# Gated linear attention in a two-layer decoder: states of 128-token tiles in place of the scores of the two largest levels

## The chip, the cores and the metric

The kernel runs on one core of a Trainium2 chip. PE (TensorE) multiplies matrices into PSUM, DVE (VectorE) and ACT (ScalarE) work on elements, POOL (GpSimd) fills masks and SP (SyncE) issues most loads. Each engine works through its own instructions in order, and semaphores hold it where data or a buffer is not ready. The metric is the device time of one execution in microseconds, the median of the runs shown.

## The reference

A trunk of two layers on 512 tokens of width 1024: latent attention, then gated linear attention (GLA), each followed by a squared-ReLU MLP of width 4096. Only GLA matters here. It has 4 heads, with 128 key channels and 256 value channels each:

```python
b = cumsum(gk)                                   # log decay, per key channel
o_inter = (q_ * exp(b_)) @ state
attn[t, s] = sum_d q_[t, d] * k_[s, d] * exp(b_[t, d] - b_[s, d])     # s <= t
o_intra = attn @ v_
new_state = state * exp(b_last) + (k_ * exp(b_last - b_)).T @ v_
...
o = rms_norm(o, g_norm) * silu(g)
```

The reference goes by chunks of 64 tokens with a state. In exact arithmetic any division into chunks gives the same output, from scores between all pairs of tokens (no state) to a state after each token.

## The kernel before, in words

Nearly every product is done in three matmuls on a high and a low part of both operands (`mm3`, L109: high by high, high by low, low by high, 32-bit words in the reduced format that the code calls F32R). `split` (L102) makes the two parts: ACT copies the high one, DVE subtracts it from the source for the low one. Products that are not split run in full f32 and leave two matmul records for each instruction. Transposes (`tr`, L128) are PE instructions against an identity.

`gla` (L1008) projects `q`, `k`, `v` and `g` from the normalized input. `q` and `k` stand with channels on partitions and tokens along the row, `v` and `g` with tokens on partitions. `b_type` (L1015) computes a half of `v` or `g`, two heads, into four PSUM banks, one for each tile of 128 tokens; `proj_qk` (L1066) computes two heads of `q` or `k`. `gates` (L1142) takes one head's decays: a matmul (L1144), absolute value, exponential, logarithm on ACT, and on DVE the sums over pairs, fours, and so on, which one exponential turns into the decays `T[m]` of blocks of m tokens, from m = 1 to m = 128.

`levels` (L1176) makes one head's scores with decay, level by level. `grow(m)` multiplies the queries of odd blocks and the keys of even blocks by the neighbour's decay, so that after it queries carry the decay since the start of their block of m tokens and keys the decay to its end. `pairs`, `fours` and `halves` fill the scores inside each tile of 128 tokens (matrix `A`), which `halves(64)` splits into `ADh` and `ADl`. `large(1)` and `large(2)` (L1267) make the scores between tiles: 128 columns for neighbouring tiles (0 to 1, 2 to 3), then 256 columns for tiles 0 and 1 against 2 and 3, in f32, each split into `AOh` and `AOl`. `apply` (L1298) multiplies scores by values: ten tile pairs of three matmuls of 256 columns, for four outputs in two PSUM banks. Each output is squared on ACT with its sum (L1312) and multiplied by the gate `g` on DVE (L1314); `small_rstd` (L273) and L1317 to L1322 scale it. `gather` (L1325) turns it to channel-major, splits it, and the output projection takes it.

The order: `heads` (L1351) yields small stages for heads 0 and 1, then for 2 and 3; each stage's products are issued behind the next stage's preparation. `proj` runs the projections in the order `v g q k G V` (capitals are the second halves, heads 2 and 3), and the loop at L1380 takes `PACE` = 1.27 stages for each unit of projection. The scores of a pair of heads can be made as soon as their `q` and `k` are there; `apply` also waits until their half of `v` and `g` is ready (`ready`, L1365). For heads 2 and 3 this is when the last projection ends, so what is left runs by itself, followed by the output projection (`out_proj`, L776). `gates(2)` and `gates(3)` are called ahead of the first `apply`.

PSUM has eight banks: two of tag "a", three "b", three "c" (L64). `apply` takes its two banks from "a" for even heads, "b" for odd ones; the `q` and `k` projections take "a". Scores, gates and transposes take "c". Work tiles of tag `tmp` have six buffers. Pools hand a buffer on when its last reader is done.

Of the kernel before, what the change touches and what calls it, by code (L numbers as in the profile page):

```python
# [34 lines left out]
HV = 256  # L35
# [15 lines left out]
def trunk_kernel(ctx: ExitStack, tc: tile.TileContext, t_in: dict, out: bass.AP, out_row: bass.AP):  # L51
    nc = tc.nc
    PE, ACT, DVE, POOL, SP = nc.tensor, nc.scalar, nc.vector, nc.gpsimd, nc.sync
# [5 lines left out]
    def uname(s):  # L59
        count[0] += 1  # L60
        return f"{s}_{count[0]}"
# [14 lines left out]
    def bank(tag):  # L76
        return psum["pool"].tile([P, 512], F32, tag=f"ps_{tag}", bufs=psum["banks"][tag], name=uname("ps"))
# [11 lines left out]
    def tmp(shape=(P, 512), dt=F32):  # L89
        return sb.tile(list(shape), dt, tag="tmp", bufs=6, name=uname("tmp"))  # L90
# [8 lines left out]
    def f(ap):  # L99
        return ap.bitcast(F32)  # L100

    def split(src, hi, lo, hi_eng=ACT, lo_eng=DVE, order=lambda i: i):  # L102
        if hi_eng is ACT:
            order(ACT.activation(hi, src, AF.Copy))  # L104
        else:
            hi_eng.tensor_copy(hi, src)
        lo_eng.tensor_tensor(lo, src, f(hi), ALU.subtract)  # L107

    def mm3(psum, w, x, start, stop):  # L109
        wh, wl = w  # L110
        xh, xl = x
        PE.matmul(psum, wh, xh, start=start, stop=False)  # L112
        PE.matmul(psum, wh, xl, start=False, stop=False)  # L113
        PE.matmul(psum, wl, xh, start=False, stop=stop)  # L114
# [6 lines left out]
    def act_e(*a, **k):  # L121
        with tc.issue_after(table[0].ins):
            return ACT.activation(*a, **k)
# [4 lines left out]
    def tr(psum, src):  # L128
        PE.transpose(psum, src, ident[: src.shape[0], : src.shape[0]])  # L129
# [13 lines left out]
    def cut(pair, *idx):  # L143
        return tuple(t[idx] for t in pair)
# [56 lines left out]
    def gcol(name, j):  # L201
        c = GAIN_COL[name] + j
        return gains[:, c : c + 1]
# [18 lines left out]
    class Norm:  # L222
# [30 lines left out]
        def add(self, j, src):  # L253
            self.scaled(j, src)
            self.square(src)
# [752 lines left out]
    def gla(layer, nrm, vtag, ytag):  # L1008
# [4 lines left out]
        gp = es.enter_context(tc.tile_pool(name="gla", bufs=1, reuse_waits="tile"))  # L1013
# [99 lines left out]
        p = bank("a")  # L1113
# [11 lines left out]
        V = [[None, None] for _ in range(NT)]  # L1125
# [16 lines left out]
        def gates(h):  # L1142
            p = bank("c")
            PE.matmul(p, wg[:, h * P : (h + 1) * P], av, start=True, stop=True)  # L1144
            bcol = gcol("bgk", 4 * layer + h)
            l = tmp()
            ACT.activation(l, p, AF.Abs, bias=bcol)
            m_ = tmp()
            DVE.tensor_scalar(m_, p, bcol, 0.0, ALU.add, ALU.min)
# [22 lines left out]
        AT = {}  # L1172
# [3 lines left out]
        def levels(h):  # L1176
            q, both, T, A = qk[h], qk[4 + h], B[h], A_of[h % 2]
            qd, k = both[:, :S], both[:, S:]
            at = AT[h] = {}
# [7 lines left out]
            def grow(m):  # L1187
                if m == 1:
                    DVE.tensor_tensor(qd.rearrange("p (t c) -> p t c", t=NT), q[:, :, :P], T[1].rearrange("p (t c) -> p t c", t=NT), ALU.mult)
# [74 lines left out]
                return products  # L1264


            def large(lev):  # L1267
                pairs = [(0, 0, P, 1), (2, P, P, 3)] if lev == 1 else [(0, 0, 256, 2), (1, 256, 256, 2)]
                width = 256 * lev
                p = bank("c")[:, :width]  # L1270
                for j, c, n, i0 in pairs:
                    PE.matmul(p[:, c : c + n], k[:, j * P : (j + 1) * P], qd[:, i0 * P : i0 * P + n], start=True, stop=True)  # L1272
                ao = tuple(gp.tile([P, width], F32R, tag=f"{x}{lev}", bufs=2, name=uname(x)) for x in ("AOh", "AOl"))
                ACT.activation(ao[0], p, AF.Copy)
                DVE.tensor_tensor(ao[1], p, f(ao[0]), ALU.subtract)
                for j, c, n, i0 in pairs:
                    for r in range(n // P):
                        at[(j, i0 + r)] = cut(ao, slice(None), slice(c + r * P, c + (r + 1) * P))

            yield pairs  # L1280
            for grown, level in (
                ((2,), lambda: fours(2)),
                ((4, 8), lambda: fours(8)),
                ((16, 32), lambda: halves(32)),
                ((64,), lambda: halves(64)),
                ((P,), lambda: lambda: large(1)),
                ((2 * P,), lambda: lambda: large(2)),
            ):
                def stage(grown=grown, level=level):
                    for m in grown:  # L1290
                        grow(m)
                    return level()

                yield stage

        Y = [None] * ND

        def apply(h):  # L1298
            at = AT[h]
            hf, vs = h // 2, slice((h % 2) * HV, (h % 2 + 1) * HV)  # L1300
            banks = [bank("ab"[h % 2]) for _ in range(2)]
            ms = sb.tile([P, NT], F32, tag="gms", bufs=2, name=uname("gms"))
            os_ = []
            for i in range(NT):
                o = banks[i // 2][:, (i % 2) * HV : (i % 2 + 1) * HV]
                for j in range(i + 1):
                    mm3(o, at[(j, i)], cut(V[j][hf], slice(None), vs), j == 0, j == i)
                os_.append(o)
                if i % 2:
                    for r in (i - 1, i):  # L1310
                        sq = tmp((P, HV))
                        ACT.activation(sq, os_[r], AF.Square, accum_out=ms[:, r : r + 1])  # L1312
                        g = G[hf][:, r, h % 2, :]
                        DVE.tensor_tensor(g, os_[r], g, ALU.mult)  # L1314
                    yield
            r = small_rstd(ms, NT, 1.0 / HV)
            for i in range(NT):  # L1317
                g = G[hf][:, i, h % 2, :]
                if i % 2:
                    ACT.activation(g, g, AF.Copy, scale=r[:, i : i + 1])  # L1320
# [30 lines left out]
        def heads():  # L1351
            for h in (0, 2):
                while any(i not in qk for i in (h, h + 1, 4 + h, 5 + h)):
                    yield
                late = None
                for two in zip(levels(h), levels(h + 1)):
                    for stage in two:
                        products = stage()
                        if late:
                            late()  # L1360
                        late = products
                        yield
# [52 lines left out]
    for k0, k1 in ((0, 1), (1, 2), (2, 4), (4, 6), (6, 8)):  # L1415
        w = piece(raw0[:, k0:k1], k1 - k0, KL, tc.keep_in_program_order)
# [160 lines left out]
```

## Time and profile before

| | |
|---|---|
| median of 3 runs | 1086.14 us |
| lowest and highest | 1085.81 and 1086.2 us |
| span of the profiled execution | 1084.4 us |
| PE busy | 1075.7 us (99%) |
| PE weight loads busy | 909.5 us (84%) |
| DVE busy | 859.6 us (79%) |
| ACT busy | 549.2 us (51%) |
| three matmuls of `mm3`, 512 columns, tiles `set`, `wh`, `wl` | 760 each, 390 to 391 ns a record |

Times in the profile are microseconds from the start of the span. A row of a timeline gives start, duration, engine, line, operation, output<-inputs and shapes. A row of a group gives the count, then busy microseconds and mean nanoseconds of one, then idle time before and what ended it. PE records overlap: the next matmul starts 0.23 us after one of 512 columns although each is shown with 0.39, so costs on PE are read from start to start. A row of windows gives the stretch, its length, the busy time of PE, of weight loads, DVE, ACT and POOL (with instruction counts), the granted PE clock, DMA's busy share and GB/s. A row of the chain of waits gives start, time and what set the end there.

### The profile page before, as it was taken

The numbers are of one execution on the slowest core, as the hardware profiler recorded it, in microseconds if no ns is written. First come the engines' busy times: TensorE is split into PE (matmuls) and PEld (weight loads), VectorE is DVE, ScalarE is ACT, GpSimd is POOL, SyncE is SP. The second block draws the span as 40 slices with busy tenths as digits, with TensorE's granted clock in tenths as the row PEclk, the third lists the DMA queues.
The fourth block names the chain that finished last, engine by engine and source line by source line (L and its number), as shares of the span: only waits on it lengthen the run. The fifth ranks groups of instructions, "written<-read, shape, count | busy, mean of one in ns | idle before, by whom it ended". The sixth has DMA issues, their size and how long they took to land.

```text
span 1084.4 us, 14045 instructions
## 1 busy us (share of the span) xinstructions
PE 1075.7 (99%) x5372; PEld 909.5 (84%) x5372; DVE 859.6 (79%) x1426; ACT 549.2 (51%) x927; POOL 43.4 (4%) x72
## 2 busy tenths in 40 slices
PE   9999999999999999999999999999999999999997
PEld 7888888888888888888788888888888888888886
DVE  7899968987887887977686584569888797797875
ACT  7767654553453453455345736556445345344354
POOL 8310002000000000000000000000000000000000
PEclk9999999999999999999999999999999999999999
DMA  7311232142332332322322222232233233223122
GB/s 225 88 50 39 79 117 78 61 134 78 117 117 78 117 117 78 110 84 79 90 76 78 78 78 75 70 127 67 90 115 119 79 101 123 87 80 125 69 97 78
DMA packets 86195, 101.61 MB, mean 94 GB/s; under 512 B 7440, under 2 KB 64016, under 8 KB 86128
## 3 DMA queue, kind: packets, MB, share of 16 engines
q1 hardware_dynamic: 84320, 99.67, 28.5%
q10 hardware_dynamic: 1808, 1.05, 0.3%
q8 instruction: 42, 0.69, 0.3%
q14 instruction: 25, 0.20, 0.1%
HBM read 98.35 MB, written 2.10 MB: 93 GB/s over the span
## 4 chain that ended last, share of the span: by engine, by line
PE 97%; DVE 1%; DMA 0%; ACT 0%; issue 0%; SPq 0%; DVEq 0%; ACTq 0%
PE ps L112 21%; PE ps L114 21%; PE ps L113 21%; PE ps L923 17%; PE ps L924 9%; PE ps L1201 2%; PE ps L129 1%; PE ps L408 1%; PE ps L871 1%; PE ps L1272 0%; PE ps L671 0%; PE ps L1251 0%; PE ps L667 0%; PE ps L670 0%; DMA gains<-in_gains_dram 0%; PE ps L669 0%
## 5 line engine op out<-in xcount | busy, mean ns | idle before, releaser
L112 PE MATMUL ps<-set,wh 128*128 128x512 f32 x760 | 296.8, 391 | 0.0
L113 PE MATMUL ps<-set,wh 128*128 128x512 f32 x760 | 296.6, 390 | 0.0
L114 PE MATMUL ps<-set,wl 128*128 128x512 f32 x760 | 296.3, 390 | 0.0
L104 ACT ACTIVATE wh<-wraw 128x1024 fp32r<-128x1024 f32 x139 | 147.0, 1061 | 240.8 <-PE ps L113 115.2
L107 DVE TENSOR_TENSOR wl<-wraw,wh 128x1024 fp32r<-128x1024 f32 x139 | 169.9, 1222 | 41.8 <-ACT wh L104 41.5
L114 PEld LDWEIGHTS ps<-set,wl 128*128 128x128 f32 x760 | 142.7, 188 | 30.3 <-DVE wl L107 0.2
L112 PEld LDWEIGHTS ps<-set,wh 128*128 128x128 f32 x760 | 142.7, 188 | 29.8
L113 PEld LDWEIGHTS ps<-set,wh 128*128 128x128 f32 x760 | 142.8, 188 | 27.6
L923 PE MATMUL ps<-T,wh 128*128 128x512 f32 x448 | 157.5, 391 | 0.0
L924 PE MATMUL ps<-T,wl 128*128 128x256 f32 x448 | 126.2, 282 | 0.0
L923 PE MATMUL ps<-set,wh 128*128 128x512 f32 x336 | 119.9, 397 | 0.0
L923 PEld LDWEIGHTS ps<-T,wh 128*128 128x128 f32 x448 | 84.1, 188 | 18.2
L924 PE MATMUL ps<-set,wl 128*128 128x256 f32 x336 | 94.2, 280 | 0.0
L107 DVE TENSOR_TENSOR wl<-comb,wh 128x1024 fp32r<-128x1024 f32 x42 | 51.4, 1223 | 47.7 <-ACT wh L104 47.7
L837 DVE TENSOR_TENSOR xT<-ps,xT 128x512 f32<-128x512 f32 x120 | 82.3, 686 | 7.1 <-PE ps L114 7.1
L104 ACT ACTIVATE wh<-comb 128x1024 fp32r<-128x1024 f32 x42 | 44.6, 1061 | 83.2 <-PE ps L923 81.8
L924 PEld LDWEIGHTS ps<-T,wl 128*128 128x128 f32 x448 | 84.6, 189 | 0.5
L923 PEld LDWEIGHTS ps<-set,wh 128*128 128x128 f32 x336 | 63.1, 188 | 15.1
L941 DVE TENSOR_TENSOR tmp<-ps,tmp 128x512 f32<-128x512 f32 x98 | 67.2, 686 | 0.9
L924 PEld LDWEIGHTS ps<-set,wl 128*128 128x128 f32 x336 | 63.4, 189 | 1.6
L112 PE MATMUL ps<-wh,set 128*128 128x512 f32 x144 | 58.8, 408 | 0.0
L104 ACT ACTIVATE wh<-raw 128x1024 fp32r<-128x1024 f32 x28 | 29.6, 1055 | 56.7 <-PE ps L923 55.7
(362 smaller groups left out, 1662.3 us busy)
## 6 DMA issues: line engine op xcount, KB each, us to landing
wraw<-in_mlp_w_up_dram SPq DMA_DIRECT2D x32, 1024.0 KB, 5.4
wraw<-in_mlp_w_down_dram SPq DMA_DIRECT2D x18, 1024.0 KB, 5.0
raw<-in_mlp_w_down_dram SPq DMA_DIRECT2D x14, 1024.0 KB, 5.1
wraw<-in_gla_w_in_dram SPq DMA_DIRECT2D x12, 1024.0 KB, 5.2
wraw<-in_mla_w_o_dram SPq DMA_DIRECT2D x4, 1024.0 KB, 5.2
wraw<-in_gla_w_o_dram SPq DMA_DIRECT2D x4, 1024.0 KB, 5.2
xT<-in_x_dram SPq DMA_DIRECT2D x6, 256.0 KB, 5.1
wraw<-in_mla_w_in_dram SPq DMA_DIRECT2D x3, 512.0 KB, 7.1
```

What stands on the lines that cost most here:

```text
L104: order(ACT.activation(hi, src, AF.Copy))
L107: lo_eng.tensor_tensor(lo, src, f(hi), ALU.subtract)
L112: PE.matmul(psum, wh, xh, start=start, stop=False)
L113: PE.matmul(psum, wh, xl, start=False, stop=False)
L114: PE.matmul(psum, wl, xh, start=False, stop=stop)
L129: PE.transpose(psum, src, ident[: src.shape[0], : src.shape[0]])
L408: PE.matmul(p, w[:, i, j * P : (j + 1) * P], x, start=start, stop=stop)
L837: DVE.tensor_tensor(xT[m], p, xT[m], ALU.add)
L923: PE.matmul(o.rearrange("p (h t) -> p h t", h=2), wh, x, start=start and k == 0, stop=False, skip_group_check=True)
L924: PE.matmul(o[:, :TH], wl, x[:, 0], start=False, stop=k == KH - 1, skip_group_check=True)
L941: DVE.tensor_tensor(by_tile(r), high, by_tile(r), ALU.add)
L1201: PE.matmul(p[:, t - t0], k[:, t * P : (t + 1) * P], moving[:, t], start=True, stop=True)
```

## The change

Between tiles, scores are no longer made. `turned` takes the place of `large(1)` and `large(2)`: it keeps the tiles' whole decays (`D`), splits the decayed queries of tiles 1 to 3, turns the decayed keys of tiles 0 to 2 to token-major by three transposes into one bank, and splits these. `states` multiplies the turned keys of each of these tiles by the values (three products of three matmuls), and chains them: the state after tile i is that tile's product plus the state before, decayed by `D`; each is split into high and low part. `apply` adds, to the four products on the diagonal, for tiles 1 to 3 the queries times the state before. The growth of decays to 256 tokens is gone. `heads` calls `states` for both heads of a pair once their values are ready, and `gates(2)`, `gates(3)` now stand ahead of `apply(0)` and `apply(1)`, behind the states. The new split queries take buffers of the tag `T`; states take three buffers of a new tag `S`.

```diff
-            def large(lev):
-                pairs = [(0, 0, P, 1), (2, P, P, 3)] if lev == 1 else [(0, 0, 256, 2), (1, 256, 256, 2)]
-                width = 256 * lev
-                p = bank("c")[:, :width]
-                for j, c, n, i0 in pairs:
-                    PE.matmul(p[:, c : c + n], k[:, j * P : (j + 1) * P], qd[:, i0 * P : i0 * P + n], start=True, stop=True)
-                ao = tuple(gp.tile([P, width], F32R, tag=f"{x}{lev}", bufs=2, name=uname(x)) for x in ("AOh", "AOl"))
-                ACT.activation(ao[0], p, AF.Copy)
-                DVE.tensor_tensor(ao[1], p, f(ao[0]), ALU.subtract)
...
+            def turned():
+                at["D"] = gp.tile([P, NT], F32, tag="D", bufs=2, name=uname("D"))
+                DVE.tensor_copy(at["D"], T[P])
+                e = gp.tile([P, 2 * S], F32R, tag="T", bufs=3, name=uname("qd"))
+                at["q"] = e[:, : S - P], e[:, S : 2 * S - P]
+                split(qd[:, P:], *at["q"])
+
+                def products():
+                    p = bank("c")[:, : S - P]
+                    for i in range(NT - 1):
+                        tr(p[:, i * P : (i + 1) * P], k[:, i * P : (i + 1) * P])
+                    at["k"] = tuple(gp.tile([P, S - P], F32R, tag=x, bufs=2, name=uname(x)) for x in ("kth", "ktl"))
+                    split(p, *at["k"])
+
+                return products
...
-                ((P,), lambda: lambda: large(1)),
-                ((2 * P,), lambda: lambda: large(2)),
+                ((P,), turned),
...
+        def states(h):
+            at, v = AT[h], head_values(h)
+            first, last = bank("c"), bank("c")
+            sums = [first[:, :HV], first[:, HV:], last[:, :HV]]
+            for i, o in enumerate(sums):
+                mm3(o, tile_of(at["k"], i), v[i], True, True)
+            at["S"] = []
+            for i, o in enumerate(sums):
+                if i:
+                    s = tmp((P, HV))
+                    DVE.tensor_tensor(s, o, decayed, ALU.add)
+                    o = s
+                if i < NT - 2:
+                    decayed = tmp((P, HV))
+                    ACT.activation(decayed, o, AF.Copy, scale=at["D"][:, i + 1 : i + 2])
+                parts = gp.tile([P, 2, HV], F32R, tag="S", bufs=3, name=uname("S"))
+                split(o, parts[:, 0], parts[:, 1])
+                at["S"].append((parts[:, 0], parts[:, 1]))
...
             for i in range(NT):
-                o = banks[i // 2][:, (i % 2) * HV : (i % 2 + 1) * HV]
-                for j in range(i + 1):
-                    mm3(o, at[(j, i)], cut(V[j][hf], slice(None), vs), j == 0, j == i)
-                os_.append(o)
+                add(i, at[(i, i)], v[i], i % 2 == 0, i == 0)
+            for i in range(NT):
+                if i:
+                    add(i, tile_of(at["q"], i - 1), at["S"][i - 1], False, True)
                 if i % 2:
...
-                if h == 0:
-                    gates(2)
-                    gates(3)
                 for r in (h, h + 1):
+                    states(r)
+                    yield
+                for r in (h, h + 1):
+                    if h == 0:
+                        gates(2 + r)
                     yield from apply(r)
```

`head_values(h)` and `tile_of(pair, i)` only cut slices, and `add` is `mm3` on one of the four outputs, all of which now lie in their banks from the start.

More of the change, by code (lines that the diff above doesn't have):

```diff
@@ L1296, in gla, with head_values, tile_of, add @@
         Y = [None] * ND
+        def head_values(h):
+            vs = slice((h % 2) * HV, (h % 2 + 1) * HV)
+            return [cut(V[j][h // 2], slice(None), vs) for j in range(NT)]
+        def tile_of(pair, i):
+            return cut(pair, slice(None), slice(i * P, (i + 1) * P))
+        def states(h):
[16 more added lines that the diff above has]
+                at["S"].append((parts[:, 0], parts[:, 1]))
         def apply(h):
-            at = AT[h]
-            hf, vs = h // 2, slice((h % 2) * HV, (h % 2 + 1) * HV)
+            at, v = AT[h], head_values(h)
+            hf = h // 2
             banks = [bank("ab"[h % 2]) for _ in range(2)]
             ms = sb.tile([P, NT], F32, tag="gms", bufs=2, name=uname("gms"))
-            os_ = []
+            os_ = [banks[i // 2][:, (i % 2) * HV : (i % 2 + 1) * HV] for i in range(NT)]
+            def add(i, w, x, start, stop):
+                for n, (a, b_) in enumerate(((w[0], x[0]), (w[0], x[1]), (w[1], x[0]))):
+                    PE.matmul(os_[i], a, b_, start=start and n == 0, stop=stop and n == 2, skip_group_check=True)
             for i in range(NT):
-                o = banks[i // 2][:, (i % 2) * HV : (i % 2 + 1) * HV]
-                for j in range(i + 1):
-                    mm3(o, at[(j, i)], cut(V[j][hf], slice(None), vs), j == 0, j == i)
-                os_.append(o)
+                add(i, at[(i, i)], v[i], i % 2 == 0, i == 0)
+            for i in range(NT):
+                if i:
+                    add(i, tile_of(at["q"], i - 1), at["S"][i - 1], False, True)
                 if i % 2:
```

3 lines of the change are left out of this document (removed).

## The prediction

> **What bounds the kernel now.** I read the page first, then the windows of the linear-attention stage, then single rows of the timeline.
>
> ```profile
> span 1084.4 us, 14045 instructions
> ...
> PE 97%; DVE 1%; DMA 0%; ACT 0%; issue 0%; SPq 0%; DVEq 0%; ACTq 0%
> ...
> wraw<-in_gla_w_in_dram SPq DMA_DIRECT2D x12, 1024.0 KB, 5.2
> ```
>
> ```profile
> 600.00:617.00 17.00, 17.00 (x98) 14.79 (x97) 11.76 (x34) 13.50 (x29) 0.00 (x0) 1.00 0.28 95
> 523.00:746.00 223.00, 222.74 (x1096) 187.19 (x1095) 151.45 (x307) 114.13 (x208) 0.00 (x0) 1.00 0.26 82
> ```
>
> 97% of the chain that ended last is matmuls, and in the whole stage (523 to 746 us) PE is busy 222.74 of 223 us at a granted clock of 1.00. So each matmul saved there is worth its start-to-start time, and each new wait of PE is paid in full. DVE (151 us) and ACT (114 us) have room on average; they matter only as chains that PE waits for. Profile and median: 1084.4 us is the profiled span, 1086.14 the median, so 1.74 us lie around the span. I keep that.
>
> **Scores away, transposes in.** Rows of the chain of waits, and the groups by shape:
>
> ```profile
> 581.09 0.45 PE ps L1272 x4
> ...
> 624.35 1.31 PE ps L129 x12
> ...
> 671.20 0.87 PE ps L1272 x4
> ```
>
> ```profile
> L1272 PE MATMUL ps<-qk 128*128 128x256 f32 x16 | 4.0, 379 | 0.0
> L1272 PE MATMUL ps<-qk 128*128 128x128 f32 x16 | 2.4, 274 | 0.0
> ```
>
> A score of 128 or 256 columns leaves two records. Four records take 0.45 us on the chain at 128 columns and 0.87 us at 256. There are 16 of each, four heads together: 4 x 0.45 + 4 x 0.87 = 5.28 us go. Three 128x128 transposes for each head come; twelve transposes of this form lie on the chain for 1.31 us. Net -3.97 us.
>
> ```profile
> 671.04 1.03 PE L1272 MATMUL ps<-qk 128*128 128x256 f32 x4
> 671.72 0.58 PE L112 MATMUL ps<-wh,set 128*128 128x512 f32 x1
> 672.14 0.40 PE L113 MATMUL ps<-wl,set 128*128 128x512 f32 x1
> 672.37 0.40 PE L114 MATMUL ps<-wh,set 128*128 128x512 f32 x1
> ```
>
> The matmul behind a block of 256-column scores starts its successor 0.42 us later, the next one 0.23 us. There are three such blocks (both heads of the first pair share one), so 3 x 0.19 = 0.57 us more go. Saving: 4.5 us.
>
> ```profile
> L129 PE MATMUL ps<-ident,g 128*128 128x128 f32 x32 | 4.2, 275 | 0.1
> ```
>
> Each transpose is shown with 275 ns, but twelve of them end in 1.31 us, 0.11 each, because they overlap. The Trainium skill ("TensorE: Matmul & The Clock Gate", Part 4: PE-mode transpose) gives about 275 ns in a kernel's context and says that access latency dominates it; charged serially, that would make 12 x 0.275 = 3.3 us and the sum 2.0 us worse. The row has the same duration, but its starts are 0.11 us apart, so the trace speaks against the serial reading; I take 0.11.
>
> The number of 256-column products stays: 30 for each head before (ten blocks of three), then 9 in `states`, 12 on the diagonal and 9 on the states. Nothing is saved there.
>
> **What lies beside PE.** For each head DVE loses one growth of the decays and two low parts of scores, and gains `D`, the low parts of `q` and turned `k`, two sums and three low parts; ACT gains five copies of 256. At about 0.4 us each that is some 2 us more on each engine for a head, 8 us in a stage with 72 us (DVE) and 109 us (ACT) free. I cost it at nothing under PE's projection matmuls; in chains it is priced below. SP's loads of `gla_w_in` wait for the same weight splits as before; these move by 1 to 3 us, and a load lands in 5.2 us while each weight chunk feeds 48 matmuls of 0.23 us, so that stays hidden. `gates(2)` and `gates(3)` move behind the states; their matmuls stay, the decays they make are first needed behind the `k` projection, 48 matmuls or 11 us later, but their ACT and DVE work now stands in the queue ahead of `apply`.
>
> **The new chains.** Prices:
>
> ```profile
> L1314 DVE TENSOR_TENSOR g<-ps,g 128x256 f32<-128x256 f32 x16 | 6.6, 422 | 3.4 <-ACT tmp L1312 3.3
> L1312 ACT ACTIVATE tmp<-ps 128x256 f32<-128x256 f32 x16 | 6.0, 379 | 4.1 <-DVE g L1314 2.2 <-PE ps L114 1.7
> L1320 ACT ACTIVATE g<-g,srstd 128x256 f32<-128x256 f32 x8 | 3.6, 502 | 2.4 <-DVE srstd L285 2.4
> L1312 ACT ACTIVATION_READ_ACCUMULATOR tmp<-ps 128x1 f32 x16 | 3.2, 198 | 0.0
> L1149 DVE TENSOR_SCALAR tmp<-ps,gains 128x512 f32<-128x512 f32 x4 | 3.0, 748 | 7.2 <-ACT tmp L1147 7.2
> L123 ACT ACTIVATE tmp<-tmp,one_t 128x512 f32<-128x512 f32 x4 | 2.9, 719 | 0.0
> L1147 ACT ACTIVATE tmp<-ps,gains 128x512 f32<-128x512 f32 x4 | 2.7, 682 | 2.6 <-PE ps L1144 2.6
> L1208 ACT ACTIVATE q<-qk 128x256 f32<-128x256 f32 x4 | 1.7, 435 | 0.3 <-DVE qk L1189 0.3
> ```
>
> ```profile
> 540.59 0.69 DVE tmp L1122
> ```
>
> ```profile
> 540.87 0.39 PE L114 MATMUL ps<-set,wl 128*128 128x512 f32 x1
> 541.33 0.50 PE L1144 MATMUL ps<-tmp,tmp 96*128 96x512 f32 x1
> 541.66 0.40 PE L112 MATMUL ps<-set,wh 128*128 128x512 f32 x1
> ```
>
> High part of a state: 0.38 us from PSUM (the square's row), 0.43 from SBUF; decayed copy 0.50; sum or low part 0.42. A matmul that had to wait (541.33) keeps its successor 0.33 us away in place of 0.23, so each real wait costs 0.1 more. That DVE step ended at 541.28, so a handover takes 0.05. All queues keep the order of the built program. No row prices a chained state itself; I add these steps in that order.
>
> *First pair of heads* (clock of the trace before; the first state product stands where `gates` stood, 599.9). ACT is free at 602.1, when this table load ends:
>
> ```profile
> 600.83 1.28 ACT L119 ACT_TABLE_LOAD   x1
> 602.12 0.69 ACT L1147 ACTIVATE tmp<-ps,gains 128x512 f32<-128x512 f32 x1
> ```
>
> Head 0's chain ends at about 606.7, under 24 projection matmuls (5.4 us) that end at 606.4, and is first used at 609.1: free. Head 1 finds the three `S` buffers taken until head 0's products have read them (609.6). From there: first high part 610.1, low 610.5, sum 610.9, decayed 611.4, second high 611.8, second sum 611.9, third high 612.7 (behind the 0.68 of `gates(2)`'s absolute value), third low 613.5 (behind its 0.75 on DVE). PE arrives at the last state's products at 612.6 and waits 0.15, then 0.65; it ends at 613.8. The second tile of the `q` projection then needs head 0's first bank, which two squares with their sums (0.38 and 0.2 each) and two multiplies release, the second multiply behind a subtraction that waits for the gate's logarithm (0.72): 615.3, a wait of 1.5 us. With 0.3 for restarts: 2.6 us. Bounds: 1.4 (the bank comes free as the states end) to 3.6 (one more 0.5 link twice).
>
> *Start of the second `v` half.* Its third bank waits for the third Silu copy of `g`, which now stands on ACT behind the split of the decayed queries and of the diagonal. These have 384 and 512 columns, 0.5 and 0.6 us between the 0.43 of 256 columns and the 0.72 of 512; the Silu itself is near 0.7. PE has six matmuls (1.4 us) to set against 1.8 to 1.9: 0.5 us, between 0 (the splits done early) and 1.2 (one step more ahead).
>
> *Second pair, after the last projection.* Here no projection covers anything:
>
> ```profile
> 688.28 0.28 PE L112 MATMUL ps<-set,ADh 128*128 128x256 f32 x1
> 689.06 1.05 ACT L104 ACTIVATE wh<-wraw 128x1024 fp32r<-128x1024 f32 x1
> 690.15 1.23 DVE L107 TENSOR_TENSOR wl<-wraw,wh 128x1024 fp32r<-128x1024 f32 x1 [0.20 <-ACT wh L104]
> 692.25 0.79 DVE L1314 TENSOR_TENSOR g<-ps,g 128x256 f32<-128x256 f32 x2 [0.54 <-ACT tmp L1312]
> ...
> 695.25 0.28 PE L114 MATMUL ps<-set,ADl 128*128 128x256 f32 x1
> ```
>
> 60 products take 7.1 us, 0.118 each. In the new order a weight split stands ahead of the chain on both engines, as it stood ahead of the squares. Head 2: decayed 690.5, first high 690.8, low 691.7, sum 692.1, decayed 692.6, second high 693.0, third high 693.6, low 694.1. Head 3 follows in the same queues: first high 693.9, low 694.4, sum 694.8, decayed 695.35, second high 695.7, second low 696.2, third high 696.4 (behind a square of head 2), third low 696.9 (behind a multiply). PE loses 0.3 on head 2, comes to head 3's second state at 694.85, and waits 0.9, 0.4 and 0.4; the 60 products end at 697.2 and not at 695.4. The output projection then waits 0.4 for head 2's bank, and head 3's transposes about 0.4 for its normalization, which is late by the same amount: 2.7 us. Bounds: 1.7 (both last waits hidden by the 0.23 us matmuls between) to 4.0 (0.1 more at each of 13 links).
>
> Sum: -4.5 + 2.6 + 0.5 + 2.7 = +1.3 us. Span 1085.7, and with 1.74 around it **1087.4 us**. A measurement of this kernel can tell about 0.2% (2.2 us) from no change, and this lies within it.
>
> **Rivals.**
> (a) *The waits are covered: faster.* Projection matmuls cover the first pair and the `v` half, and of the end only the 1.8 us by which the products run late are left: -4.5 + 1.8 = -2.7, 1083.4. For it: DVE and ACT have much room on average. Against: PE's order is fixed, and the bank of the second `q` tile is named in it behind head 0's multiplies.
> (b) *The chains set the end: slower.* Place: the states of the two later heads (1 and 3), whose three `S` buffers are head 0's and 2's. Price: with 0.1 us more at each of some 25 links in both places, 2.5 us more, 1089.9. It decides from 0.9 us more, 0.035 a link. For it: 600 to 617 us has ACT busy 13.50 of 17 already. Against: the handover from engine to engine shows 0.05 us, which I have put in.
> (c) *The transposes cost what their duration says*, 2.0 us more: 1089.4. Against it the chain row, twelve in 1.31 us. The serial reading of the Trainium skill's figure, above, would be this case.
> (d) *It moves work and changes nothing for PE*: the 256-column products are 120 before and after, so if transposes took the scores' time, only the waits were left: 1086.14 + 5.8 = 1091.9. The rows exclude most of it.
>
> **How the numbers follow.** Forecast as worked out: 0.51. (a) 0.12, (b) 0.30, (c) 0.05, (d) 0.02. The forecast's own range is 1085.0 to 1088.3. Faster by over 0.2% is below 1083.97: most of (a), 0.12. Slower is above 1088.31: (b), (c), (d), 0.37. The rest, 0.51, is no change. The range 1084.8 to 1090.2 leaves out the better part of (a) and the tail of (b) and (d).
>
> **What would show it.** Transposes of `qk` near 0.11 us apart and no L1272 rows confirm the saving. In the timeline of PE, gaps of 0.7 to 1.6 us near 612 to 615 (minus the 2.6 us saved before them), with the DVE multiply of `g` as the releaser of the later one, confirm the first pair; gaps of 0.4 to 1 us at the second and third state of the last head confirm the end. I am wrong if ACT or DVE steps of 256 columns take over 0.5 us, if PE shows no such gaps, or if one over 2 us stands anywhere else in the stage.

## The result, and the profile after

| | before | changed |
|---|---|---|
| median (lowest to highest), 20 runs each | 1086.16 us (1085.75 to 1086.97) | 1088.16 us (1086.56 to 1089.38) |
| changed / before | | 1.0016, 95% interval 1.001 to 1.0023 |
| span of the profiled execution | 1084.4 us | 1087.3 us |

The time lies 0.8 us above the forecast, inside its range; the ratio's estimate is within the 0.2% that were called no change, its interval reaches just beyond. But the runs of the changed kernel don't lie around their median: ten are at 1086.56 to 1087.78 us and ten at 1088.54 to 1089.38 us. Before, all 20 lie within 1.3 us. The profiled execution (1089.12 us) is one of the upper ten.

The page after, its groups by shape, and the linear-attention stage in the view of windows:

```profile
span 1087.3 us, 14050 instructions
...
L112 PE MATMUL ps<-set,wh 128*128 128x512 f32 x760 | 297.4, 391 | 1.4 <-DVE g L1347 1.2
```

```profile
L1335 PE MATMUL ps<-S,qd 128*128 128x256 f32 x36 | 6.6, 294 | 1.1 <-ACT S L104 0.6 <-DVE S L107 0.4
L129 PE MATMUL ps<-ident,qk 128*128 128x128 f32 x12 | 2.0, 271 | 0.0
```

```profile
523.00:746.00 223.00, 220.06 (x1066) 183.03 (x1065) 153.60 (x323) 117.80 (x225) 0.00 (x0) 0.99 0.25 82
```

No L1272 row is left. PE is idle 2.9 us in the stretch in which it was idle 0.26 us before, and the releasers are the predicted ones: the parts of a state on ACT and DVE (L104, L107) and the multiply by `g` (L1347). What was not predicted is the clock, 0.99 in place of 1.00. PE's timeline after the products of head 0 shows where:

```profile
612.19 0.50 PE L1335 MATMUL ps<-S,qd 128*128 128x256 f32 x2 [0.43 <-DVE S L107]
613.94 0.50 PE L112 MATMUL ps<-set,wh 128*128 128x512 f32 x1 [1.24 <-DVE g L1347]
...
615.48 0.63 PE L114 MATMUL ps<-set,wl 128*128 128x512 f32 x1
615.91 0.63 PE L112 MATMUL ps<-set,wh 128*128 128x512 f32 x1
616.34 0.63 PE L113 MATMUL ps<-set,wh 128*128 128x512 f32 x1
...
618.04 0.52 PE L114 MATMUL ps<-set,wl 128*128 128x512 f32 x1
618.40 0.40 PE L112 MATMUL ps<-set,wh 128*128 128x512 f32 x1
```

The two waits of the first pair stand at 612 and 614 us, as forecast. Read from start to start they cost 0.70 and 1.40 us (the idle figure in brackets counts from the modelled end of the record before). Then matmuls of 512 columns start 0.43 us apart, not 0.23, until 618.3 us, and nothing is named in brackets: PE isn't waiting, it is slow. The windows of the same execution, cut where its clock changes (columns as before; the granted clock stands behind POOL's):

```profile
608.06:611.47 3.41, 3.41 (x28) 3.13 (x27) 1.92 (x5) 2.22 (x6) 0.00 (x0) 1.00 0.85 268
611.47:614.89 3.42, 1.75 (x8) 1.20 (x8) 3.09 (x9) 2.39 (x10) 0.00 (x0) 1.00 0.12 44
614.89:618.30 3.41, 3.41 (x10) 2.62 (x9) 3.29 (x15) 3.41 (x11) 0.00 (x0) 0.50 0.00 0
618.30:621.71 3.41, 3.41 (x16) 2.78 (x16) 1.52 (x4) 2.51 (x8) 0.00 (x0) 1.00 0.00 0
```

For 3.41 us the clock is granted at half, right behind a window of the same length in which PE was busy 1.75 us only. At half clock 3.41 us do the work of 1.7.

At the end of the stage:

```profile
696.81 1.66 PE L1335 MATMUL ps<-S,qd 128*128 128x256 f32 x6 [0.55 <-ACT S L104]
698.59 0.50 PE L112 MATMUL ps<-set,wh 128*128 128x512 f32 x1
```

The first row holds the six products with head 3's second and third state. By starts PE loses 0.71 us ahead of it, 0.37 and 0.21 within the six, and 0.29 ahead of the output projection.

All of it by kinds, worked out from the starts of all matmuls between the first gates matmul (L1144) and the first of the second MLP (L923), each matmul counted until the next one starts. The third column is an execution of the changed kernel without the stretch at half clock, from the runs below:

| us, start to start | before | changed, profiled | changed, full clock |
|---|---|---|---|
| scores, 128 and 256 columns | 1.46 + 2.90 | 0 | 0 |
| transposes of keys (12) | 0 | 0.98 | 0.98 |
| 256-column products (120) | 14.44 | 18.46 | 18.46 |
| 512-column matmuls (780) | 182.61 | 184.24 | 182.66 |
| `halves` (32) | 3.22 | 3.33 | 3.32 |
| the rest | 17.51 | 17.48 | 17.46 |
| sum | 222.13 | 224.49 | 222.89 |

So the change costs 0.76 us in this stage at full clock and 2.36 us with the half clock. The other 0.5 us between the two profiled spans (2.9 us) lie ahead of the stage, where the code is the same.

### The profile page after: what moved, and what is told of

Read it like the earlier page. It is cut to its first block, busy times and chain, and to the rows that moved or that the text cites. A ratio compares the mean times of both kernels' runs of the same rounds, so it can differ in the third digit from the quotient of the medians.

```text
span 1087.3 us, 14050 instructions
## 1 busy us (share of the span) xinstructions
PE 1076.4 (99%) x5352; PEld 908.3 (84%) x5352; DVE 865.1 (80%) x1446; ACT 554.9 (51%) x947; POOL 42.1 (4%) x72
## 5 line engine op out<-in xcount | busy, mean ns | idle before, releaser
L104 ACT ACTIVATE wh<-wraw 128x1024 fp32r<-128x1024 f32 x139 | 147.0, 1061 | 235.0 <-PE ps L113 115.6
L107 DVE TENSOR_TENSOR wl<-wraw,wh 128x1024 fp32r<-128x1024 f32 x139 | 169.8, 1223 | 36.8 <-ACT wh L104 36.6
L923 PE MATMUL ps<-T,wh 128*128 128x512 f32 x448 | 157.5, 391 | 0.0
L923 PE MATMUL ps<-set,wh 128*128 128x512 f32 x336 | 119.9, 397 | 0.0
L923 PEld LDWEIGHTS ps<-T,wh 128*128 128x128 f32 x448 | 84.1, 188 | 18.2
L107 DVE TENSOR_TENSOR wl<-comb,wh 128x1024 fp32r<-128x1024 f32 x42 | 51.3, 1223 | 47.0 <-ACT wh L104 46.9
L104 ACT ACTIVATE wh<-comb 128x1024 fp32r<-128x1024 f32 x42 | 44.6, 1061 | 83.3 <-PE ps L923 81.8
L923 PEld LDWEIGHTS ps<-set,wh 128*128 128x128 f32 x336 | 63.1, 188 | 15.1
L104 ACT ACTIVATE wh<-raw 128x1024 fp32r<-128x1024 f32 x28 | 29.5, 1054 | 56.7 <-PE ps L923 55.8
```

Of the source, the lines that this page charges most:

```text
L923: PE.matmul(o.rearrange("p (h t) -> p h t", h=2), wh, x, start=start and k == 0, stop=False, skip_group_check=True)
```

## The experiments

Times are medians; each was compared with runs of the kernel before on its chip, whose medians were 1086.42 us (e1, e3, e4, e6, on one chip), 1086.40 us (a2, e7, e9, e10, on a second) and 1086.27 us (e2, e5, e11, e12, on a third). "Stage" is the sum of the table above, against 222.13 us before.

My theory after the first look: the waits of the first pair (2.1 us) come from head 1's state buffers and from the gates' work in the queues of ACT and DVE, the half clock from these waits, the 1.6 us at the end from the length of the chains, and the saving is about what was predicted. Each part has its rivals in the expectations.

**Only one pair by states** (e3, e4, and e3's kernel again as e12). Each keeps `large(1)`, `large(2)` and the old `apply` for the other pair:

```diff
-                ((P,), turned),
+                *([((P,), turned)] if h // 2 in (0,) else
+                  [((P,), lambda: lambda: large(1)), ((2 * P,), lambda: lambda: large(2))]),
```

> States for heads 2 and 3 only; heads 0 and 1 keep the scores between tiles (the gates stand as in the changed kernel, the first ahead of apply of head 0, the second ahead of that of head 1). My theory: 2.6 + 0.4 - 0.65 = 2.35 us saved, 1.6 us lost in waits at the end of the stage: 1085.4, with the clock at full speed throughout and runs as close together as before the change (within 1.3 us). Rival 1, the half clock comes from something else than the waits of the first pair: runs spread over 3 us as with the changed kernel, some at 1087.2. Rival 2, the end costs the 2.7 us that I predicted: 1086.5.

Measured: 1085.70 us (1085.31 to 1086.43, 11 runs), stage 221.56, the clock at 1.00 and no gap in the first pair. One group, within 0.3 us of the expected time: rival 2 falls. Against rival 1 the trace speaks more than the runs, since e3, on the same chip, has the waits and one group too.

> States for heads 0 and 1 only; heads 2 and 3 keep the scores between tiles. My theory: of the saving 2.6 + 0.2 - 0.65 = 2.2 us are left, the first pair's waits of 2.1 us stay, and so does the stretch at half clock behind them in about half of the runs; the end of the stage is as before the change. 1086.2 at full clock, 1088.0 with the half clock; two groups of runs. Rival 1, the end of the stage carries the loss and the first pair is covered: 1084.0, one group. Rival 2, the saving is smaller than the rows say (1 us less): 1086.7 and 1088.5.

> The kernel with states for heads 0 and 1 only, once more. It has the same two waits in the first pair as the changed kernel (0.69 and 1.40 us), but none of its 11 runs stood apart. My theory: whether the half clock comes depends on how the waits lie in a raster of 3.413 us that starts with the program's clock, which is chance; 3 to 7 of 11 runs near 1089.4, the others near 1087.9. Rival: the waits alone are not enough, something in the changed kernel that this one lacks is needed; then again one group near 1087.9, and I can't name the condition.

Measured: e3 1087.96 us (1087.50 to 1088.45, 11 runs), one group; e12, the same program on another chip, 1089.55 us: four runs at 1087.64 to 1088.31, seven at 1089.43 to 1090.12. Both traces have the waits of 0.7 and 1.4 us. The lower group lies 1.7 us above my number. Most of it is accounted for: in this mixed kernel the second pair's scores wait 0.55 us for a bank between `large(1)` and `large(2)`, 0.35 us is a wait in the levels and 0.2 us a part of the saving counted twice (both below), and the kernel before stands 0.26 us higher in this set. As for the groups, e12 is as the theory expects; that e3 showed none in 11 runs on its chip stays unexplained, and for that reason one group in e1, e4 and e6, which ran on e3's chip, doesn't show by itself that the half clock is gone.

**The half clock** (e6, a2). e6 adds products that nobody reads, where PE waits (`fill` issues n of them, here cut):

```diff
...
+                if h == 1 and i == 3:
+                    fill(at, 2)
                 if i:
                     add(i, tile_of(at["q"], i - 1), at["S"][i - 1], False, True)
+                if h == 1 and i == 3:
+                    fill(at, 6)
```

> The changed kernel with eight products more, of 384 columns, whose result nobody reads: two ahead of the products with head 1's third state and six behind, about 1.4 us of PE in the two places where it waits. My theory: they fit into the waits (2.1 us), PE isn't idle there, the clock stays at full speed, and all runs are within 1 us around 1087.3, without the group at 1089. Rival 1, the half clock isn't caused by these waits: the two groups stay, 1087.3 and 1089.1. Rival 2, the waits are no spare time, and the products come on top: 1088.6 and 1090.5.

Measured: 1087.44 us (1086.91 to 1087.85, 11 runs). One group, at the place of the lower one. The stage takes 222.87 us, as without the products at full clock, so they fit into the waits; a wait of 0.61 us is left:

```profile
612.20 0.63 PE L1329 MATMUL ps<-qd,kth 128*128 128x384 f32 x2
612.67 0.40 PE L1340 MATMUL ps<-S,qd 128*128 128x256 f32 x2
612.90 0.87 PE L1329 MATMUL ps<-qd,kth 128*128 128x384 f32 x4
614.22 0.50 PE L112 MATMUL ps<-set,wh 128*128 128x512 f32 x1 [0.45 <-DVE g L1356]
```

That these products also remove the upper group isn't shown by the runs alone, as e3 has none there either. In the trace of e6 no window of the stage comes near what is followed by a half clock elsewhere (last section). In run times the comparison to go by is that of a2 and e10 below, on one chip: with waits of 2.1 us the runs spread over both groups, with 0.29 us left there is one.

> The changed kernel itself once more, beside the others. My theory: its runs fall into two groups again, near 1087.1 and near 1089.0, and the profiled execution is either one with a stretch of 3.4 us at half clock behind the waits of the first pair (span near 1087.3) or one without (span near 1085.3, clock at full speed to the end); the two differ by 1.6 us of matmuls of 512 columns. Rival 1: the groups have another cause; an execution near 1087 shows the half clock too, or one near 1089 doesn't. Rival 2: the half clock depends on the chip or the day and not on the waits: one group only.

Measured: 1088.02 us (1086.72 to 1089.13, 11 runs), again spread over both groups. Its profiled execution (span 1085.2) has the same two waits, and no half clock. The windows, on the raster on which its clock rose at the start:

```profile
609.81:613.22 3.41, 2.00 (x14) 1.52 (x12) 2.99 (x7) 3.28 (x11) 0.00 (x0) 1.00 0.52 201
613.22:616.63 3.41, 3.16 (x14) 2.63 (x15) 3.29 (x15) 2.51 (x9) 0.00 (x0) 1.00 0.00 0
```

In every trace here the clock is at full speed for a whole multiple of 3.413 us (607.57 us before the half clock of the changed kernel is 178 times that), so it is decided on a raster. Here the end of the second wait falls into the next window (613.22 to 613.47 us); in the execution above both waits lie in one. Span 1085.2 against 1087.3, and in the table 182.66 against 184.24 in the 512-column matmuls alone, 1.58 us.

**Buffers or gates in the first pair** (e1, e10, e2).

```diff
-                parts = gp.tile([P, 2, HV], F32R, tag="S", bufs=3, name=uname("S"))
+                if h == 1:
+                    parts = slot(vtag).rearrange("p (a b) -> p a b", a=2)
+                else:
+                    parts = gp.tile([P, 2, HV], F32R, tag="S", bufs=3, name=uname("S"))
```

> The three states of head 1 get buffers of their own (free tiles of the values' slots), so that they no longer wait until head 0's products have read the three S buffers; all else as in the changed kernel. My theory: the 0.7 us at head 1's state products go, but the second tile of the q projection still waits for head 0's first bank, whose second multiply by g stands behind the gates' work; PE comes there earlier and waits longer. Of the 2.1 us of both waits 1.4 to 2.1 stay: 1086.5 to 1087.4 in the runs with full clock. Rival 1, the S buffers set everything there: both waits go, 1085.0. Rival 2, the order of ACT and DVE changes nothing and neither wait depends on buffers: 1088.2 as the changed kernel. In runs with the half clock of 3.4 us all these are 1.7 to 1.9 us higher.

Measured: 1086.04 us (1085.48 to 1086.64, 11 runs), one group, stage 221.42. One wait of 0.96 us is left of 2.1. This is better than I expected and not as good as rival 1. ACT's rows, of the changed kernel and of e1, show why: the high part of head 1's first state,

```profile
608.37 0.39 ACT L104 ACTIVATE S<-ps 128x256 fp32r<-128x256 f32 x1 [1.86 <-PE ps L1335]
```

```profile
605.76 0.37 ACT L104 ACTIVATE set<-ps 128x256 fp32r<-128x256 f32 x1
```

no longer waits for a product (L1335) that reads the old buffer, and starts 2.6 us earlier, 2.0 counted from the start of the stage (541.85 and 541.23 us). What stands behind it in the queues, the gates and the squares, moves up with it, so the second wait shrinks too; I had left that wait in its place.

```diff
                 for r in (h, h + 1):
+                    yield from apply(r)
                     if h == 0:
                         gates(2 + r)
-                    yield from apply(r)
```

> The gates of heads 2 and 3 are called behind the products of heads 0 and 1 instead of ahead of them; all else as in the changed kernel. My theory: the 1.4 us wait of the second tile of the q projection hangs on the gates' work ahead of the squares and multiplies on ACT and DVE, so it shrinks to 0.4 or less, the 0.7 us at head 1's state stay (S buffers); no half clock, since the wait that is left is short: 1085.7 to 1086.2, one group. Rival 1: the bank is late from the chains themselves and the wait stays: 1087.1 and 1089 in two groups. Rival 2: the late decays are missed later, at the fine levels of heads 2 and 3: a new wait of 1 us or more there, 1086.9.

Measured: 1085.27 us (1084.75 to 1085.66, 11 runs), ratio 0.999 (0.9981 to 0.9999), stage 220.89. Of both waits 0.29 us are left, though the S buffers are as in the changed kernel. DVE in the changed kernel and here, between two multiplies by `g` of head 0:

```profile
612.24 0.42 DVE L1347 TENSOR_TENSOR g<-ps,g 128x256 f32<-128x256 f32 x1
612.86 0.69 DVE L1154 TENSOR_TENSOR T<-tmp,tmp 128x512 f32<-128x512 f32 x1 [0.19 <-ACT tmp L123]
613.47 0.42 DVE L1347 TENSOR_TENSOR g<-ps,g 128x256 f32<-128x256 f32 x1
```

```profile
610.34 0.42 DVE L1347 TENSOR_TENSOR g<-ps,g 128x256 f32<-128x256 f32 x1
610.67 0.42 DVE L107 TENSOR_TENSOR S<-tmp,S 128x256 fp32r<-128x256 f32 x1
611.30 0.79 DVE L1347 TENSOR_TENSOR g<-ps,g 128x256 f32<-128x256 f32 x2 [0.21 <-ACT tmp L1345]
```

The gates' subtraction (L1154), which waits for a logarithm, is gone from between them, and the second multiply starts 2.2 us earlier, 1.9 counted from the start of the stage (541.85 and 541.62 us). The 0.7 us that I expected to stay with the S buffers went too, so the time is below my range: in the changed kernel the last links of that chain stand behind the gates' absolute value on ACT and its counterpart on DVE, as the prediction had walked them.

e2 calls `gates(2)` and `gates(3)` ahead of the states, where they stood before the change.

> The gates of heads 2 and 3 are called where they were before the change, ahead of everything that waits for the values, so ahead of the states; all else as in the changed kernel. My theory: their work, some 3 us on ACT and 3 us on DVE for each head, then stands ahead of the chains in both queues; the chains of heads 0 and 1 come 2 to 4 us later than with the gates behind, and PE waits 1.5 to 4.5 us there instead of 2.1, in other places: 1086.5 to 1089.5, more in runs with the half clock. Rival 1, what costs is only that the gates stand between states and multiplies: then the waits shrink as with the gates behind the products, 1085.3, one group. Rival 2, the place of the gates doesn't matter: 1087.1 and 1088.9 in two groups.

Measured: 1090.62 us (1090.10 to 1091.87, 5 runs), stage 227.22 in the profiled execution:

```profile
612.50 0.38 PE L1335 MATMUL ps<-S,qd 128*128 128x256 f32 x1 [0.73 <-ACT S L104]
613.32 1.04 PE L1335 MATMUL ps<-S,qd 128*128 128x256 f32 x5 [0.44 <-DVE S L107]
615.37 0.79 PE L112 MATMUL ps<-set,wh 128*128 128x512 f32 x1 [1.01 <-DVE g L1347]
```

```profile
611.16:614.58 3.42, 2.03 (x10) 1.20 (x8) 3.35 (x12) 1.76 (x6) 0.00 (x0) 1.00 0.60 228
614.58:617.99 3.41, 2.62 (x6) 2.14 (x7) 2.51 (x12) 3.31 (x15) 0.00 (x0) 0.50 0.00 0
617.99:621.40 3.41, 3.41 (x9) 2.64 (x9) 2.54 (x11) 1.93 (x8) 0.00 (x0) 0.50 0.00 0
```

Waits of 0.29, 0.89, 0.70 and 1.17 us by starts, 3.05 in all, and a half clock that lasts two windows. No run of the five lies in a lower group. Both rivals fall: the place of the gates matters, ahead of the states is the worst of three, behind the products the best.

**The end of the stage** (e11, e7).

```diff
+                if h == 3:
+                    parts = gp.tile([P, NT * 192], F32R, tag="q", bufs=3, name=uname("S"))[:, : 2 * HV].rearrange("p (a b) -> p a b", a=2)
```

> Only the three states of head 3 get buffers of their own (free tiles of the tag q); all else as in the changed kernel. My theory: in the trace of the changed kernel the steps of head 3 follow those of head 2 in the queues of ACT and DVE without waiting for a buffer, so the waits of 0.7, 0.4, 0.2 and 0.3 us at the end of the stage stay: 1087.1 and 1088.9, as the changed kernel. Rival 1, the three S buffers hold head 3 up, as in my case of the chains that set the end: 1 us or more less, 1086.1 and 1087.8.

Measured: 1088.84 us (1087.12 to 1089.31, 11 runs), the waits at the end 0.76, 0.37, 0.21 and 0.29 us as in the changed kernel. The S buffers play no part there.

e7 issues each tile's state product from `v_done`, one tile late (both branches give t - 1; the body, here cut, is that of `states` for heads 2 and 3):

```diff
                 V[t][hf] = (hi, lo)
+                if hf == 1 and t:
+                    for i in (t - 1,) if t < NT - 1 else (t - 1,):
+                        early(i)
...
+        def early(i):
+            p = bank("c")
+            for n, h in enumerate((2, 3)):
...
+                mm3(o, tile_of(at["k"], i), v, True, True)
```

> For heads 2 and 3 each tile's state product is issued as soon as the tile's values are evacuated, that is between the tiles of the last projection, both heads in one bank, and the states of head 3 lie in free tiles of the tag q, not in the S buffers. The first pair is as in the changed kernel. My theory: the 1.6 us of waits at the end of the stage go but for 0.2: 1085.5 at full clock, 1087.2 with the half clock behind the first pair. Rival 1: the chain itself is too long for what covers it, or ACT with the evacuations holds it up: 0.8 us or more stay, 1086.3 and 1088. Rival 2: the products between the tiles delay the projection by a wait for a bank: 1087.1 or more and 1089.

Measured: 1087.44 us, from 1085.84 to 1088.58 (11 runs; four lie below 1086.1), stage 221.75 in an execution at full clock. The waits at the states are gone; ahead of the output projection 0.57 us are left, where I had 0.2. Of the 1.58 us, 1.0 went: the chains were too late, not too long.

**The price of the scores** (e5). The old score matmuls are issued again ahead of the transposes, into banks that nobody reads:

```diff
                 def products():
+                    s = bank("c")
+                    for c, j, n, i0 in ((0, 0, P, 1), (P, 2, P, 3)):
+                        PE.matmul(s[:, c : c + n], k[:, j * P : (j + 1) * P], qd[:, i0 * P : i0 * P + n], start=True, stop=True)
+                    s = bank("c")
+                    for j in range(2):
+                        PE.matmul(s[:, j * 256 : j * 256 + 256], k[:, j * P : (j + 1) * P], qd[:, 256:], start=True, stop=True)
```

> The changed kernel with the old score matmuls between tiles still issued (the same 16 instructions of 128 and of 256 columns, in f32, ahead of the transposes), into banks that nobody reads. My theory, by starts of the matmuls in the trace before: they cost 1.46 + 2.90 = 4.4 us, and up to 0.6 more by what follows them; with the waits as they are 1091.5 to 1092.1, and a second group 1.6 us higher. Rival 1, the rows of the chain, by which I predicted, are right: 5.3 + 0.6 = 5.9 us, 1093.0. Rival 2, they fill time in which PE waits for other engines: under 3.5 us, 1090.6 or less.

Measured: 1094.65 us (5 runs: 1092.95 and 1093.13, then 1094.65 to 1094.89), stage 230.29 with the half clock, 5.80 above that of the changed kernel with it. The time is rival 1's, but by another sum: 0.61 us are waits for a bank and their restart (0.51 and 0.10), which the old place of the scores didn't have. The 32 records start 0.11 and 0.22 us apart, 16 x 0.112 + 16 x 0.216 = 5.25 us. So 5.3 for the matmuls was right, and my 4.4 by starts too low, because of what the last score of each block hands on (next section).

**All three** (e9): e1's, e7's and e10's edits in one.

> The three edits in one: buffers of their own for head 1's states, the gates of heads 2 and 3 behind the products of heads 0 and 1, and the states of heads 2 and 3 issued between the tiles of the last projection. My theory: of the waits only some 0.3 us are left, and the saving of 3.4 us on scores and transposes shows: 1083.2 to 1083.8, one group, faster than both kernels. Rival 1: the saving is smaller and was made up by other work: 1085 or more though the waits are gone. Rival 2: the waits come back elsewhere (decays late at the fine levels of heads 2 and 3, or a bank): 1084.5 to 1086, with a gap over 0.7 us in the trace.

Measured: 1083.63 us (1083.21 to 1084.47, 11 runs), ratio 0.9976 (0.9967 to 0.9985), the fastest here and faster than both kernels. Stage 219.39: 256-column products 15.18, 512-column matmuls 182.78. The largest wait left is 0.58 us by starts, at the output projection's first matmul:

```profile
690.95 1.46 PE L1366 MATMUL ps<-S,qd 128*128 128x256 f32 x11
692.83 0.50 PE L112 MATMUL ps<-set,wh 128*128 128x512 f32 x1 [0.41 <-DVE g L1378]
```

The saving is there, and the changed kernel loses it in its waits: both rivals fall.

## Why the prediction was right, and where it wasn't

**The saving, -4.5.** 5.25 us for scores (e5's records) less 1.31 for twelve transposes at 0.11 is the -3.97 that I had, within 0.03. The 0.57 us that I took off besides was counted twice. In the rows quoted in the prediction, the last score of a block of 256 columns begins at 671.69, 0.03 us ahead of the next matmul, which then holds its successor 0.42 us and not 0.23. Those 0.19 us are the fourth score's own time, and the 0.87 us for four records already contained them. The table shows it from the other side: by starts the scores take 4.36 us, and 0.9 us of theirs stand in the row of 512 columns (3 x 0.19 and 4 x 0.085). The transposes, in the timeline of the changed kernel:

```profile
672.82 0.49 PE L129 MATMUL ps<-ident,qk 128*128 128x128 f32 x3
673.06 0.47 PE L112 MATMUL ps<-wh,set 128*128 128x512 f32 x1
673.37 0.39 PE L113 MATMUL ps<-wl,set 128*128 128x512 f32 x1
```

Three take 0.24 us to the next matmul's start and hand on 0.08 (0.31 in place of 0.23): 0.11 each. Rival (c), 0.275 each in series, falls, and (d) with it.

**First pair, +2.6.** Right in mechanism and size: waits of 0.70 and 1.40 us (0.65 and 1.5 worked out), with the releasers named. e1 bears out that the three `S` buffers start head 1's chain late, e10 that the gates' work in the queues makes the rest: either edit alone takes away the first wait and part of the second. The wait of 0.15 didn't come. Behind each of the two waits a matmul holds its successor 0.11 us longer than usual (0.22 us at 612.19, 0.34 at 613.94), where I had 0.3 for restarts, so the pair costs 2.3 us.

**Start of the second `v` half, +0.5.** Right place and releaser, too large. PE and ACT in the changed kernel:

```profile
667.83 0.39 PE L114 MATMUL ps<-wh,set 128*128 128x512 f32 x1
668.24 0.50 PE L112 MATMUL ps<-wh,set 128*128 128x512 f32 x1
```

```profile
666.44 0.51 ACT L104 ACTIVATE qd<-qk 128x384 fp32r<-128x384 f32 x1
666.86 0.62 ACT L104 ACTIVATE ADh<-A 128x512 fp32r<-128x512 f32 x1
667.50 1.27 ACT L1052 ACTIVATE g<-ps,rtok 128x512 f32<-128x512 f32 x2
```

The matmul at 668.24 is the first into the third bank, six behind the first of the half. It starts 0.05 us after the third Silu copy (0.69 us from 667.50), which stands behind the two splits as worked out; nothing waits for that copy in the kernel before. By starts this is 0.18 us, and 0.11 for the restart. What the prediction didn't have is a longer wait 4.3 us earlier, in the levels of heads 2 and 3, whose copy on ACT (L1243) comes behind the first two Silu copies:

```profile
663.95 0.39 PE L112 MATMUL ps<-wh,set 128*128 128x512 f32 x1
664.52 0.71 PE L1251 MATMUL ps<-E 128*128 128x128 f32 x4 [0.19 <-ACT E L1243]
```

0.35 us by starts. With what else is new in the rows of 512 columns and `halves` this comes to about 0.7 us (182.66 - 182.61 + 0.9 - 0.33 for the transposes' own share there, and 0.10). Of these 0.2 are restarts of the two pairs, so 0.5 are left. That is the size that was forecast, but by luck: only 0.3 lie at the place that was named.

**Second pair, +2.7.** Right place, too large: 1.58 us, 1.9 with the restarts (the terms as listed add up to 2.8). I had 0.9, 0.4 and 0.4 at head 3's states, where 0.71, 0.37 and 0.21 stand, 0.29 in place of 0.4 ahead of the output projection, and head 3's transposes didn't wait. e11 leaves the case of the buffers (rival b, its second place) without support.

**The sum.** +1.3 was predicted; the stage shows +0.76 at full clock, so the errors partly cancelled: 0.57 too much saved, and 5.3 us on the two pairs where 4.2 came (4.0 in the 256-column products, 0.2 behind them). **The missing step** is the clock. The prediction read the granted clock as 1.00 in the trace before and kept it, though the change brought waits of 2.1 us within 3 us. In about half of the runs that costs 1.6 us more, which moves the median to 1088.16; the ten lower runs, 1086.56 to 1087.78, lie around the forecast. That the upper ten come near rival (b)'s 1089.9 isn't by (b)'s cause: the links at the end of the stage are no longer than worked out (high parts 0.37 to 0.41 us, sums and low parts 0.41 to 0.42, decayed copies 0.46 to 0.51).

## What to carry to other kernels

When work is chained across engines, look at what stands ahead of each link in the in-order queues of the helpers: moving the gates behind the products was worth 2.0 us here at full clock, half of what the change saves on scores. A short wait can cost more than its length, since the clock may follow; two groups of runs with the same trace but for a slow stretch are the sign. And count a matmul either from start to start or from the chain's row, never both, because the last one of a block hands part of its time to its neighbour.

## What was unexpected of the hardware

The clock went to half after waits of 2.1 us in two pieces, not after a long stop. The busy time in one window of the 3.413 us raster looks as if it told the executions apart: with weight loads busy 1.20 us (the changed kernel, and e2) the next window ran at half clock, with 1.52 (a2) it did not, nor with 1.47 in e11:

```profile
610.50:613.92 3.42, 1.96 (x14) 1.47 (x12) 3.01 (x7) 3.24 (x11) 0.00 (x0) 1.00 0.50 193
```

But at the end of the program before the change a window with 1.09 us of weight loads is followed by one at full clock, in which PE has nothing to do:

```profile
1076.35:1079.77 3.42, 1.72 (x8) 1.09 (x6) 1.06 (x5) 1.19 (x4) 0.00 (x0) 1.00 0.39 153
1079.77:1083.18 3.41, 0.00 (x0) 0.00 (x0) 0.93 (x3) 0.51 (x1) 0.00 (x0) 1.00 0.40 154
```

Nor does the busy time of the matmuls part them (2.03 in e2 with half clock, 1.96 in e11 without); their ends are modelled. A count by starts does. Give each matmul the time until the next one starts, but at most 0.227 us for 512 columns and in proportion for fewer, and add this up in every window of the raster at full clock, in all 14 traces. The ten windows with the least, up to 1.25 us, are each followed by half clock (1.06 in the changed kernel, 0.93 in e2, and windows at the end of programs); all others, from 1.31 us up, by full clock (1.33 in e11, 1.38 in a2, 1.55 in the first row above). So the border lies, by this count, between 1.25 and 1.31 us of 3.413; that it is columns streamed which count, and not something that goes with them, no run tests.

What a kernel risks can be read from one trace by sliding the raster over it. In the changed kernel (ten of twenty runs in the upper group) two fifths of all positions put a window under the border on the first pair's waits, in e2 every position, in e1, e4, e6, e9 and e10 none (their least windows of the stage hold 1.46 us or more). That fits which of these had an upper group. The Trainium skill ("TensorE: Matmul & The Clock Gate", Part 1) describes this window of 3413 ns, free-running, and has the half clock in its table of the two states as what comes after at least one idle window. The length and the raster agree with the traces; that a whole window must be idle does not. Open is why e3, with the same two fifths, had no such run of eleven on its chip, while e12 had seven.
